# Adding the weights by DMA onto the negated high part, for every second weight piece of the mixer phases

## The chip, the cores and the metric

The kernel runs on one core of a Trainium2 chip. The metric is the time of one execution on the device in microseconds (us): 961.36 us in the median of three runs (961.18 to 961.63). Beside these times there is one profiled execution, whose trace gives the instructions of each engine: TensorE (PE, with its weight loads PEld), VectorE (DVE), ScalarE (ACT), GpSimd (POOL) and SyncE (SP, which only issues DMAs here).

## The reference

Two layers of a decoder trunk work on 272 positions (16 learned ones and 256 of the sequence) of width 1024, all in float32. Cut to what matters:

```
for l in range(2):
    h = rms_norm(x, norm1_g[l])
    u = h @ w_in[l]                      # conv, q, kv, rope key, recurrence inputs, 3 x 1024 gates
    A = conv_module(u_conv) @ w_conv_out[l]     # GLU, causal depthwise conv k=31, layer norm, swish
    B = mla(c_q, c_kv, k_rope) @ w_attn_out[l]  # causal attention, 8 heads
    C = hgrn2(q, f, i, g) @ w_hgrn_out[l]       # gated linear recurrence, in chunks, 4 heads
    mix = sig(gA) * A + sig(gB) * B + sig(gC) * C
    x = x + mix @ w_out[l]
    x = x + square(relu(rms_norm(x, norm2_g[l]) @ w_ff1[l])) @ w_ff2[l]
return x[:, 16:]
```

## The kernel before

Activations lie transposed in SBUF: 128 partitions of features by 272 columns of positions (256 in parts of the second layer). The weights stay in HBM and come in pieces of 128x1024 float32, 512 KiB each; one piece holds eight 128x128 blocks.

The large products keep the accuracy of float32 by three products of a shorter format, float32r. Every operand is split into a high part (the value rounded to float32r) and a low part (the value less the high part). `mm3` multiplies, for each block, high by high (L219), weights low by high (L220), and high by activations low (L221).

`piece` (L204) makes a weight piece ready in three steps. `fetch` (L104) loads it into a buffer `wraw` through SP's DMA queue (L106). ACT rounds it into `whi` (L209). DVE subtracts, `wraw` less `whi`, into `wlo` (L211). There are three `wraw` buffers and four each of `whi` and `wlo`. A buffer of `whi` or `wlo` is free again when the matmuls that read it are done, one of `wraw` when its last reader is done.

Each layer has two phases. In the mixer phase, `win_acc` multiplies 51 pieces of w_in (piece j = 0 is the rope key and goes another way; j = 1 to 7 are the latents and the recurrence queries, j = 8 to 27 the other inputs, j = 28 to 51 the 24 gate tiles). `merge_tile` multiplies 12 pieces of the three branch matrices (wbr), each piece serving two of its 24 tiles, scales by the gate (L996) and sums (L998). The other work of the mixers is written as four step generators: `latent_steps`, `hgrn_steps` (the recurrence, with the products of L840 and L844), `attention_steps` and `conv_steps` (the convolution, 31 taps for each of four channel groups on DVE, L931 and L935). A loop over a list of the dense tiles draws steps from them at fixed rates. The list is the 20 head tiles j = 8 to 27, 15 gate tiles, and then a merge tile and, as long as there are any, a gate tile by turns. Before the first merge tile of a branch its generator is run to its end.

In the second phase come 8 pieces of w_out, 32 of w_ff1 and 32 of w_ff2, with no other large work beside them.

Every engine works through its own instructions strictly in their order, and waits at the first whose inputs or buffer are not ready. This order is made when the program is built: a planner plays the program through with its own costs of each instruction and gives each engine, whenever it comes free, the ready instruction of the highest priority. Priority is the order of writing, moved ahead by `tc.high_priority`: by 500 for `piece`, by 300 to 400 for the steps of recurrence, attention and latents, by nothing for the convolution. So a change of one instruction can move others.

POOL does small things: memsets of the recurrence's buffers (`kl`, L799), copies (`qm`, L851) and powers for the norms (L238, L912). It issues no DMA.

Of the kernel before, what the change touches and what calls it, by code (L numbers as in the profile page):

```python
# [10 lines left out]
F32 = mybir.dt.float32  # L11
# [3 lines left out]
AF = mybir.ActivationFunctionType  # L15
# [24 lines left out]
NLAT = 8  # L40
# [46 lines left out]
def block_kernel(ctx, tc, xT_d, pp_d, cc_d, win_d, wuq_d, wukv_d, wbr_d, wout_d, wff1_d, wff2_d, out_d):  # L87
    nc = tc.nc
    pe, act, dve, pool = nc.tensor, nc.scalar, nc.vector, nc.gpsimd
    MUL, ADD, SUB = ALU.mult, ALU.add, ALU.subtract  # L90
# [13 lines left out]
    def fetch(src, n=1024):  # L104
        raw = wsp.tile([P, 1024], F32, name="wraw", tag="wraw")
        nc.sync.dma_start(out=raw[:, :n], in_=src[:, :n])  # L106
        return raw
# [3 lines left out]
    with tc.high_priority(offset=2 * AHEAD):  # L111
        nc.scalar.dma_start(out=pp, in_=pp_d)
        for j in range(4):
            nc.sync.dma_start(out=xT[:, 2 * j:2 * j + 2, :], in_=xT_d[:, 2 * j:2 * j + 2, :])
            if j == 0:
                first = {"kr": fetch(win_d[0, 0], KD * ROPE), "kv": fetch(win_d[0, 1])}
# [72 lines left out]
    def psum_acc():  # L189
        return ps_acc.tile([P, 512], F32, name="acc", tag="acc")  # L190
# [4 lines left out]
    def psum_hx():  # L195
        return ps_hx.tile([P, 512], F32, name="hx", tag="hx")
# [4 lines left out]
    def psum_sm():  # L201
        return ps_sm.tile([P, 512], F32, name="sm", tag="sm")

    def piece(src, raw=None):  # L204

        with tc.high_priority(offset=AHEAD):
            raw = raw or fetch(src)
            hi = wsp.tile([P, 1024], F32R, name="whi", tag="whi", bufs=4)
            act.copy(out=hi, in_=raw)  # L209
            lo = wsp.tile([P, 1024], F32R, name="wlo", tag="wlo", bufs=4)  # L210
            dve.tensor_tensor(out=lo, in0=raw, in1=hi.bitcast(F32), op=SUB)  # L211
        return hi, lo

    def split(hi, lo, src):
# [3 lines left out]
    def mm3(out, whi, wlo, xhi, xlo, start, stop):  # L218
        pe.matmul(out, whi, xhi, start=start, stop=False)  # L219
        pe.matmul(out, wlo, xhi, start=False, stop=False)  # L220
        pe.matmul(out, whi, xlo, start=False, stop=stop)  # L221
# [62 lines left out]
    def scale_input(xg, l, k):  # L284
# [16 lines left out]
                      in1=lb[:, 5, :].unsqueeze(1).broadcast_to([P, 2, HH]), op=MUL)  # L301
# [5 lines left out]
    for l in range(DEPTH):  # L307
# [33 lines left out]
        def unit(name, dt=F32):  # L341
            return t4.tile([P, HH, L], dt, name=name, tag="u")
# [22 lines left out]

        tiles = win_tiles()
        def win_acc(j, n0):
            hi, lo = piece(win_d[l, j], first["kv"] if l == 0 and j == 1 else None)
            xh, xl = xg if j < NLAT else (hhi, hlo)
            ps = psum_hx() if j < NLAT and j % 2 == 0 else psum_acc()  # L370
            for k in range(KD):
                o = k * P
                mm3(ps[:, :L - n0], hi[:, o:o + P], lo[:, o:o + P], xh[:, k, n0:], xl[:, k, n0:],
                    k == 0, k == KD - 1)
            return ps
# [22 lines left out]
        def head_tile(j):  # L398
            kind, i, _, _ = tiles[j]
            if kind == "kr":  # L400
                rope_keys(j)
                return
            n0 = T0 if kind in ("q", "g") else 0
            ps = win_acc(j, n0)[:, :L - n0]
            with tc.high_priority(offset=200):
                take(kind, i, ps, n0)
# [40 lines left out]
        def latent_steps():  # L447
# [44 lines left out]
            for g in range(2):  # L492
                uqhi, uqlo = piece(wuq_d[l, g])
                for h in range(4):
                    ps = psum_mx()[:, :L]
                    for j in range(2):
                        o = j * 512 + h * P
                        mm3(ps, uqhi[:, o:o + P], uqlo[:, o:o + P], cqhi[:, j, :], cqlo[:, j, :], j == 0, j == 1)
                    act.activation(out=msq_[:QK, h, :], in_=ps[:QK], func=AF.Square)
                    dve.tensor_tensor(out=qT[g][:, h, :], in0=ps, in1=csg, op=MUL)  # L500
                    yield
                with together():
                    for h in (3, 2, 1, 0):
                        pe.matmul(sums[32 * h:32 * h + 32, :L], sel96[:QK, g, :], msq_[:QK, h, :], start=(g == 0), stop=(g == 1))
                yield
# [3 lines left out]
            for w in qtiles:  # L509
# [10 lines left out]
                                     in1=heads(ra[:, 1, q0:3]), op0=MUL, op1=MUL)  # L520

            ukhi, uklo = piece(wukv_d[l])
            kT = [unit(f"kT{g}") for g in range(2)]
            vv = [half(f"vv{w}", "vv", 3) for w in range(3)]
# [449 lines left out]
        mix = {}  # L974

        def gate_tile(i):

            ps = win_acc(N_HEAD_TILES + i, T0)
            gates[i] = gp.tile([P, L], F32, name="gate", tag="gate")
            act.activation(out=gates[i][:, :N], in_=ps[:, :N], func=AF.Tanh, scale=0.5)  # L980

        def merge_tile(i):
            b, m = divmod(i, KD)
            yh, yl = ys[BRANCHES[b]]
            if i == 0:
                mix["sum"] = [unit(f"mix{j}") for j in range(2)]
            if i % 2 == 0:
                mix["w"] = piece(wbr_d[l, i // 2])
            bhi, blo = mix["w"]
            ps = (psum_acc, psum_hx, psum_hx)[b]()  # L990
            for k in range(4):
                o = (i % 2 * 4 + k) * P
                mm3(ps[:, :N], bhi[:, o:o + P], blo[:, o:o + P], yh[:, k, T0:], yl[:, k, T0:], k == 0, k == 3)
            g, total = gates[i], mix["sum"][m // 4][:, m % 4, :N]
            with tc.high_priority(offset=AHEAD):
                dve.scalar_tensor_tensor(out=total if b == 0 else g[:, :N], in0=g[:, :N], scalar=1.0, in1=ps[:, :N], op0=ADD, op1=MUL)  # L996
            if b > 0:
                dve.tensor_tensor(out=total, in0=total, in1=g[:, :N], op=ADD)  # L998
            if b == 2:
                if m == 0:  # L1000
                    mix["hi"] = actp.tile([P, KD, L], F32R, name="mhi", tag="ahi")
                    mix["lo"] = actp.tile([P, KD, L], F32R, name="mlo", tag="alo")
                act.activation(out=mix["hi"][:, m, T0:], in_=total, func=AF.Copy, scale=0.5)
                dve.scalar_tensor_tensor(out=mix["lo"][:, m, T0:], in0=total, scalar=0.5, in1=mix["hi"][:, m, T0:].bitcast(F32),
                                         op0=MUL, op1=SUB)
# [3 lines left out]
        for i in range(3 * KD):  # L1009
            dense.append((merge_tile, i))  # L1010
            if i + NGATE < 3 * KD:
                dense.append((gate_tile, i + NGATE))
# [193 lines left out]
```

## Time and profile before

| | |
|---|---|
| three runs | 961.18, 961.36, 961.63 us |
| the profiled execution | 961.29 us, of which the span from its first to its last instruction is 959.5 us |
| granted TensorE clock | 0.991 of full speed over the span |
| PE busy | 931.0 us, 97% |
| DVE busy | 716.5 us, 75% |
| ACT busy | 526.3 us, 55% |
| POOL busy | 50.7 us, 5% |
| DMA | 149.16 MB, HBM read 146.91 MB |

Times in the rows are in us unless they stand as ns. Matmuls overlap, so "PE busy" can be full while their number per us still varies. A line such as "out<-in x276 | busy, mean ns | idle <-releaser" gives a group of instructions by the program's names, their count, their busy time in all, the mean of one, and the idle time of the engine just before them with what ended it. Layer 0's mixer phase lies at about 0 to 276 us, layer 1's at about 480 to 752 us.

### The profile page before, as it was taken

The numbers are of one execution on the slowest core, as the hardware profiler recorded it, in microseconds if no ns is written. First come the engines' busy times: TensorE is split into PE (matmuls) and PEld (weight loads), VectorE is DVE, ScalarE is ACT, GpSimd is POOL, SyncE is SP. The second block draws the span as 40 slices with busy tenths as digits, with TensorE's granted clock in tenths as the row PEclk, the third lists the DMA queues.
The fourth block names the chain that finished last, engine by engine and source line by source line (L and its number), as shares of the span: only waits on it lengthen the run. The fifth ranks groups of instructions, "written<-read, shape, count | busy, mean of one in ns | idle before, by whom it ended". The sixth has DMA issues, their size and how long they took to land. (4 is left out here: it accounts for less than half of the span.)

```text
span 959.5 us, 18623 instructions
## 1 busy us (share of the span) xinstructions
PE 931.0 (97%) x7474; PEld 896.2 (93%) x7474; DVE 716.5 (75%) x1348; ACT 526.3 (55%) x945; POOL 50.7 (5%) x87
## 2 busy tenths in 40 slices
PE   6999999899999999999999999997998999999998
PEld 6899999779999999999999889896897999999998
DVE  7799999976887766555557998999668887665552
ACT  6467665554546555544445587665444566663331
POOL 3004000000000000000010021000000000000000
PEclk9999999989999999999999999998999999999999
DMA  8454433414445555555454444333144466555661
GB/s 264 131 176 140 147 133 111 133 34 142 163 148 178 194 176 177 176 176 176 160 172 158 141 145 155 130 132 113 67 146 163 155 195 199 179 190 187 198 203 56
DMA packets 42422, 149.16 MB, mean 155 GB/s; under 512 B 4704, under 2 KB 6368, under 8 KB 42336
## 3 DMA queue, kind: packets, MB, share of 16 engines
q1 hardware_dynamic: 40608, 146.10, 46.2%
q10 hardware_dynamic: 1728, 1.88, 0.6%
q8 instruction: 58, 0.95, 0.4%
q14 instruction: 28, 0.23, 0.1%
HBM read 146.91 MB, written 1.05 MB: 154 GB/s over the span
## 5 line engine op out<-in xcount | busy, mean ns | idle before, releaser
L209 ACT CAST whi<-wraw 128x1024 fp32r<-128x1024 f32 x276 | 289.3, 1049 | 340.4 <-PE acc L221 191.2
L211 DVE TENSOR_TENSOR wlo<-wraw,whi 128x1024 fp32r<-128x1024 f32 x276 | 337.6, 1223 | 167.0 <-ACT whi L209 165.4
L219 PE MATMUL acc<-hhi,whi 128*128 128x272 f32 (+1 forms) x704 | 205.1, 292 | 2.3 <-ACT scrahi L417 1.6
L221 PE MATMUL acc<-hlo,whi 128*128 128x272 f32 (+1 forms) x704 | 202.7, 289 | 0.2 <-DVE hlo L216 0.2
L220 PE MATMUL acc<-hhi,wlo 128*128 128x272 f32 (+1 forms) x704 | 202.2, 287 | 0.0
L219 PEld LDWEIGHTS acc<-hhi,whi 128*128 128x128 f32 x704 | 132.6, 188 | 6.6 <-ACT scrahi L417 1.8
L221 PEld LDWEIGHTS acc<-hlo,whi 128*128 128x128 f32 x704 | 132.4, 188 | 2.5 <-issue 0.9
L220 PEld LDWEIGHTS acc<-hhi,wlo 128*128 128x128 f32 x704 | 132.6, 188 | 1.2 <-issue 0.4
L935 DVE SCALAR_TENSOR_TENSOR cacc<-hpad,pph,cacc 128x272 f32<-128x272 f32 (+1 forms) x240 | 111.0, 485 | 0.7
L220 PE MATMUL acc<-xhi,wlo 128*128 128x272 f32 (+1 forms) x256 | 73.4, 287 | 0.0
L220 PE MATMUL hx<-xhi,wlo 128*128 128x272 f32 (+1 forms) x256 | 73.2, 286 | 0.0
L221 PE MATMUL acc<-xlo,whi 128*128 128x272 f32 (+1 forms) x256 | 73.1, 286 | 0.0
L221 PE MATMUL hx<-xlo,whi 128*128 128x272 f32 (+1 forms) x256 | 72.9, 285 | 0.0
L220 PE MATMUL hx<-fhi,wlo 128*128 128x272 f32 (+1 forms) x256 | 72.9, 285 | 0.0
L220 PE MATMUL acc<-fhi,wlo 128*128 128x272 f32 (+1 forms) x256 | 72.9, 285 | 0.0
L219 PE MATMUL acc<-fhi,whi 128*128 128x272 f32 (+1 forms) x256 | 72.8, 284 | 0.0
L219 PE MATMUL hx<-fhi,whi 128*128 128x272 f32 (+1 forms) x256 | 72.8, 284 | 0.0
L221 PE MATMUL acc<-flo,whi 128*128 128x272 f32 (+1 forms) x256 | 72.7, 284 | 0.0
L221 PE MATMUL hx<-flo,whi 128*128 128x272 f32 (+1 forms) x256 | 72.7, 284 | 0.0
L219 PE MATMUL acc<-xhi,whi 128*128 128x272 f32 (+1 forms) x256 | 72.7, 284 | 0.0
L219 PE MATMUL hx<-xhi,whi 128*128 128x272 f32 (+1 forms) x256 | 72.7, 284 | 0.0
L221 PEld LDWEIGHTS acc<-xlo,whi 128*128 128x128 f32 x256 | 48.3, 189 | 0.1
(375 smaller groups left out, 2097.3 us busy)
## 6 DMA issues: line engine op xcount, KB each, us to landing
wraw<-in_wff_dram SPq DMA_DIRECT2D x128, 512.0 KB, 3.4
wraw<-in_win_dram SPq DMA_DIRECT2D x102, 512.0 KB, 3.4
wraw<-in_wbr_dram SPq DMA_DIRECT2D x24, 512.0 KB, 3.3
wraw<-in_wout_dram SPq DMA_DIRECT2D x16, 512.0 KB, 3.3
wraw<-in_wuq_dram SPq DMA_DIRECT2D x4, 512.0 KB, 3.2
xT<-in_xT_dram SPq DMA_DIRECT2D x4, 272.0 KB, 5.4
wraw<-in_wukv_dram SPq DMA_DIRECT2D x2, 512.0 KB, 3.7
out_dram<-xT ACTq DMA_DIRECT2D x8, 128.0 KB, 2.4
```

Source lines behind the costliest of these rows:

```text
L209: act.copy(out=hi, in_=raw)
L211: dve.tensor_tensor(out=lo, in0=raw, in1=hi.bitcast(F32), op=SUB)
L219: pe.matmul(out, whi, xhi, start=start, stop=False)
L220: pe.matmul(out, wlo, xhi, start=False, stop=False)
L221: pe.matmul(out, whi, xlo, start=False, stop=stop)
L935: dve.scalar_tensor_tensor(out=a, in0=hpad[:, c, T0 + k:T0 + k + N], scalar=hpar(l, "cw", c * CK + k), in1=a, op0=MUL, op1=ADD)
```

## The change

For some pieces DVE no longer subtracts. ACT writes the negated high part into `wlo`, and a DMA issued from POOL adds the weights from HBM onto it. These are the w_in pieces with odd j from 9 on (22 in each layer) and every second wbr piece (6 in each layer).

```diff
-    def piece(src, raw=None):
+    def piece(src, raw=None, adding=False):
+
 
         with tc.high_priority(offset=AHEAD):
             raw = raw or fetch(src)
             hi = wsp.tile([P, 1024], F32R, name="whi", tag="whi", bufs=4)
             act.copy(out=hi, in_=raw)
             lo = wsp.tile([P, 1024], F32R, name="wlo", tag="wlo", bufs=4)
-            dve.tensor_tensor(out=lo, in0=raw, in1=hi.bitcast(F32), op=SUB)
+            if adding:
+                act.activation(out=lo, in_=hi.bitcast(F32), func=AF.Copy, scale=-1.0)
+                nc.gpsimd.dma_start(out=lo, in_=src, accum_op=ADD)
+            else:
+                dve.tensor_tensor(out=lo, in0=raw, in1=hi.bitcast(F32), op=SUB)
         return hi, lo
...
         def win_acc(j, n0):
-            hi, lo = piece(win_d[l, j], first["kv"] if l == 0 and j == 1 else None)
+            hi, lo = piece(win_d[l, j], first["kv"] if l == 0 and j == 1 else None, j >= NLAT and j % 2 == 1)
...
             if i % 2 == 0:
-                mix["w"] = piece(wbr_d[l, i // 2])
+                mix["w"] = piece(wbr_d[l, i // 2], adding=i % 4 == 2)
```

## Rows read from the trace of the kernel before

**Rows 1.** The page's busy times, and DVE in 40 slices of 24 us.
```profile
PE 931.0 (97%) x7474; PEld 896.2 (93%) x7474; DVE 716.5 (75%) x1348; ACT 526.3 (55%) x945; POOL 50.7 (5%) x87
...
DVE  7799999976887766555557998999668887665552
```
**Rows 2.** Busy us (x instructions) by stretch: PE, PEld, DVE, ACT, POOL; clock, DMA share, GB/s.
```profile
120.00:150.00 30.00, 30.00 (x241) 27.78 (x240) 28.01 (x69) 19.36 (x50) 0.84 (x2) 1.00 0.37 123
170.00:202.00 32.00, 26.51 (x197) 21.91 (x195) 29.66 (x79) 18.59 (x49) 0.29 (x1) 0.89 0.27 89
552.00:576.00 24.00, 22.44 (x180) 21.49 (x179) 23.00 (x45) 21.68 (x37) 5.62 (x3) 1.00 0.42 142
656.00:680.00 24.00, 18.44 (x139) 15.36 (x139) 21.26 (x57) 12.97 (x34) 0.63 (x1) 0.79 0.19 66
720.00:744.00 24.00, 20.28 (x160) 19.03 (x159) 19.76 (x40) 11.81 (x19) 0.00 (x0) 1.00 0.45 156
744.00:768.00 24.00, 24.00 (x206) 24.00 (x205) 20.34 (x40) 13.33 (x23) 0.00 (x0) 1.00 0.50 158
```
**Rows 3.** PE's waits (total, times, longest) in 160 to 215, 640 to 700, 715 to 750.
```profile
PE hx L844 <- DVE k L840: 3.3, 1, 3.3
...
PE hx L844 <- DVE k L840: 2.8, 1, 2.8
...
PE hx L219 <- DVE gate L996: 2.7, 4, 0.9
PE hx L221 <- DVE yalo L216: 1.0, 2, 0.6
```
**Rows 4.** DVE's costliest groups in 170 to 202 us.
```profile
L935 DVE SCALAR_TENSOR_TENSOR cacc<-hpad,pph,cacc 128x272 f32<-128x272 f32 x39 | 17.7, 492 | 0.1
L211 DVE TENSOR_TENSOR wlo<-wraw,whi 128x1024 fp32r<-128x1024 f32 x5 | 6.1, 1222 | 1.2 <-ACT whi L209 1.2
```
**Rows 5.** The page's groups of the two split steps.
```profile
L209 ACT CAST whi<-wraw 128x1024 fp32r<-128x1024 f32 x276 | 289.3, 1049 | 340.4 <-PE acc L221 191.2
L211 DVE TENSOR_TENSOR wlo<-wraw,whi 128x1024 fp32r<-128x1024 f32 x276 | 337.6, 1223 | 167.0 <-ACT whi L209 165.4
```
**Rows 6.** The loads' DMA queue, the landings of wraw, and ACT's waits for them.
```profile
q1 hardware_dynamic: 40608, 146.10, 46.2%
...
DMA to landing us min/median/max: 2.8/3.4/6.6
...
ACT whi L209: 7.8, 11
```
**Rows 7.** POOL in order of time, 78 to 205 us: first and last of 11.
```profile
78.86 4.29 POOL L238 TENSOR_TENSOR rq<-rq,mhalf 128x24 f32<-128x24 f32 x1 [2.83 <-DVE rq L516]
...
203.67 1.00 POOL L912 TENSOR_TENSOR ss<-ss,mhalf 16x4 f32<-16x4 f32 x1 [16.98 <-DVE ss L911]
```
**Rows 8.** ACT's roundings with PE's first low-part matmuls of their pieces, by time.
```profile
27.13 1.05 ACT L209 CAST whi<-wraw 128x1024 fp32r<-128x1024 f32 x1 [0.85 <-DMA wraw<-in_win_dram]
...
39.76 0.29 PE L220 MATMUL acc<-hhi,wlo 128*128 128x272 f32 x1
...
45.70 1.05 ACT L209 CAST whi<-wraw 128x1024 fp32r<-128x1024 f32 x1
...
50.52 0.29 PE L220 MATMUL acc<-hhi,wlo 128*128 128x272 f32 x1
...
715.17 1.05 ACT L209 CAST whi<-wraw 128x1024 fp32r<-128x1024 f32 x1 [3.60 <-PE acc L221]
716.12 0.37 ACT L980 ACTIVATE gate<-acc 128x256 f32<-128x256 f32 x1
...
721.74 0.28 PE L220 MATMUL acc<-hhi,wlo 128*128 128x256 f32 x1
...
735.85 1.04 ACT L209 CAST whi<-wraw 128x1024 fp32r<-128x1024 f32 x1 [0.70 <-PE hx L221]
...
748.99 0.28 PE L220 MATMUL hx<-yahi,wlo 128*128 128x256 f32 x1
```

## The prediction

> **What bounds the kernel now.** I read the busy times first. TensorE (PE) works 931.0 of 959.5 us, 97%; VectorE (DVE) has 75% and ScalarE (ACT) 55%, but DVE is at 7 to 9 tenths in the slices of the two mixer phases [rows 1]. So the time can move in two ways only: PE's missing time can shrink, or PE can be made to wait where it does not wait now.
>
> Second, the table by stretches [rows 2]. In 120 to 150 us PE starts 241 matmuls in 30 us (8.03 per us) while DVE works 28.01 of 30: PE is the bound and DVE is nearly full beside it. In three stretches PE falls behind: 170 to 202 us (197 matmuls; at 8.03 per us 24.5 us of work, so 7.5 us lost), 656 to 680 us (139, 17.3 us, 6.7 lost) and 720 to 744 us (160; at the 206 in 24 us of the stretch behind it 18.6, so 5.4 lost). Together 19.6 us: the most that any help for DVE can bring there. In the first two the granted clock is at 0.89 and 0.79 of full speed, a mix of the 1.2 and 2.4 GHz levels while PE idled; that loss is inside the 19.6.
>
> Third, who PE waited for in these three stretches [rows 3]: a key product of the recurrence (L840) 3.3 and 2.8 us, merge and split results (L996, L216) 2.7 and 1.0 us, all of DVE: 9.8 us. The rest are ping-pong chains and waits for ACT. What DVE does in 170 to 202 us [rows 4] shows why not all 19.6 is DVE's fault: 17.7 of its 29.7 us are convolution taps (L935), which fill holes; splits (L211) are only 6.1.
>
> **What is removed.** Each layer has 22 changed pieces of win (odd j from 9 to 51) and 6 of wbr: 56 in all. Each loses one subtraction of 1.223 us [rows 5]: 68.5 us of DVE. What it is worth is read from the stretches: I credit the 9.8 us of PE's DVE waits (these stretches hold changed pieces, and 16 splits that vanish between 60 and 202 us, 19.6 us, are more than the 17.7 us of taps, so these can be out of the way before the chains run short of dense work). Bounds: nothing (the chains stay, an ACT step is added to them) and 19.6 us.
>
> **What is added on ACT.** A negated copy of 128x1024, 56 times. The nearest row is the rounding copy of that size, 1.049 us [rows 5]; 58.7 us in all, ACT from 526 to 585 us. ACT has room nearly everywhere (19.36 of 30 us busy in 120 to 150); where it has not is 552 to 576 us, 21.68 of 24 [rows 2]. Three changed pieces (j 19, 21, 23 of layer 1) put 3.15 us into 2.32 us of room: 0.8 us, and 3.15 if it all reaches PE, 0 if some other work fills in.
>
> **What is added on the DMA queue of GpSimd (POOL).** 56 issues that read the weights again: 512 KiB each, 29.4 MB on top of the loads' 146.10 [rows 6]. The DMA engines are busy 0.37 of 120 to 150 us [rows 2], so throughput hides it; without that cover the weight loads (3.4 us to landing) would come late, for which the rounding copies wait 7.8 us in all now. POOL itself has 11 operations between 78 and 204 us, the first of them the longest, 4.29 us, with long waits before them (16.98 us before the last) [rows 7]. An issue waits at the head of POOL's stream for its negated copy, and memsets of kl and powers queue behind it; conversely an issue put behind one of those waits sits there. With so few of them I cost both at nothing; each such collision would cost up to 4.3 us. The raw buffer is freed by the rounding copy, not by the subtraction, so the next load leaves SP's queue at least 1.2 us sooner; loads are not what PE waits for, so that is worth nothing.
>
> **The path that becomes late.** Before: rounding copy, then 1.22 us of DVE, then PE. After: rounding copy, negated copy, issue, landing, PE. PE needs the low part with the second matmul of a piece. The room is the time from the end of the rounding copy to that matmul. Four buffers for the high part set it: a copy starts only when a piece three places earlier is done. Examples [rows 8]: layer 0, j 11: 46.75 to 50.52, 3.8 us; layer 1, j 51: 716.22 to 721.74, 5.5. I took it so for all 56, from the first (28.18 to 39.76, 11.6 us) to the last (736.89 to 748.99, 12.1 us): one has 3.8, one 4.9, six 5.5 to 6.0, six 6.3 to 7.2, and 42 have 8.0 or more. Dense phases have 8 to 12, the merge phases 5.5 to 8.
>
> The price of the path: negated copy 1.05; one other ACT operation that slips in between, 0.37 as the gate's tanh at 716.12 [rows 8]; 0.1 for the hand-overs between the engines, my choice; and the landing. No row shows a DMA issued from POOL, nor one that adds. Bounds from the plain load: 3.4 us at its median, if adding and reading the old value cost nothing, and 6.6, its slowest landing [rows 6]. The add moves two operands: the load's packets took 46.2% of 959.5 us for 146.10 MB, so 1.59 us for 512 KiB; 3.4 + 1.59 = 5.0, and 0.3 for sharing the engines (0.37 busy, of half of 1.59): I take 5.3. Path 1.05 + 0.37 + 0.1 + 5.3 = 6.8 us (4.6 at the low bound without the slip, 8.1 at the high one).
>
> PE's loss is the sum of path less room over the pieces with less room. At 6.8: twelve pieces, 12.7 us. At 4.6: 0.8 us. At 8.1: 30.4 us. These losses add up, since a late piece pushes its followers, and their rooms move with it.
>
> The Trainium skill, DMA: Bandwidth & Descriptors, Anatomy of one DMA, puts a DMA issued from GpSimd at about 2.0 us plus bytes over 436 thousand, an estimate of 3.2 us here. By that alone the path would be 4.7 us, the loss 0.9, and the sum 953 us; no run here shows such a DMA, and the fit is not of an adding one.
>
> **The sum.** 12.7 + 0.8 - 9.8 = +3.7 us. The profiled execution took 961.29 us (span 959.5 and 1.8 around it), the median of three is 961.36: 965 us. All bounds at their worst: 30.4 + 3.2 - 0 = +33.6 (995); at their best 0.8 + 0 - 19.6 = -18.8 (942).
>
> **The rivals.**
> *DVE's relief wins (faster).* One mechanism: the landing is at or below 4.9 us, so that the path is 6.4 and the loss 8.5, less than 9.8 - 0.8. At a path of 6.0 the loss is 5.2; with 14 us of the 19.6 given back, because the taps are out of the tails, 961.3 + 5.2 + 0.8 - 14 = 953 us. For it: 17.7 us of taps in the 32 us before the merge, 42 of 56 pieces with 8 us of room, and the order on each engine is planned anew, so other ready matmuls may stand where a late piece stood. Against: the merge phases have nothing else to run.
> *The add is much slower.* At a path of 9 us (a landing of 7.5, beyond the bound) 23 pieces are late by 47.3 us in all: 961.3 + 47.3 + 0.8 - 9.8 = 1000 us. A mechanism of this kernel would be that the issue waits for DVE: an issue that must let a running DVE operation end waits up to 1.22 us behind a split, 0.49 behind a tap, and DVE works 28.01 of 30 us; path 8.0, loss 29, 982 us. The Trainium skill, SBUF — State Buffer, SBUF: two separate sides, says that GpSimd can't write descriptors while DVE holds the shared port in its two-port mode; no run here shows it. By that rule the operations with two inputs in SBUF, which are most of DVE's here, would not do it, so I give it little.
> *It evens out.* Loss and gain within 1.9 us: 961 us, with a path of 6.3 to 6.5.
> *It doesn't do what it says* can be excluded: the subtractions leave DVE's stream.
>
> **How the numbers follow.** A modest loss, 963 to 981 us: 0.39. Relief wins: 0.36. Much slower add: 0.12. Even: 0.13. Faster by over 0.2% (1.9 us, about what a measurement of this kernel can tell) 0.36, same 0.13, slower 0.51. The forecast is 965 us. Its own case spans 963 to 981; the range goes on through the even case and most of the faster one, down to 948, and into the slow one to 988: about 0.1 is left out on each side.
>
> **What would show it.** L211 220 times instead of 276, DVE near 648 us, ACT near 585, memory reads near 176 MB. Issue to landing of the add: 5.3 us. PE's waits: a new one for this DMA at the low part, some 13 us, in the merge phases (225 to 260, 700 to 735 us); the L840, L996 and L216 waits gone. The tap count in the last 30 us before each merge falls. I am wrong if PE shows no wait for the adding DMA (landing under 5, or work put in its place), if ACT's waits in the softmax chain grow, or if the three stretches lose as much as before.

## The result

The changed kernel takes 974.70 us in the median of four runs (972.91 to 978.66), the kernel before 961.27 us beside it (960.18 to 961.63): a ratio of 1.0139, 95% interval 1.0124 to 1.0155. So it is slower by 13.4 us. The forecast was 965 us with a range of 948 to 988 and 0.51 on slower. The sign came out and the place of the loss in part; both terms of the sum were too small.

### The profile page after: what moved, and what is told of

Same layout as the page of the kernel before. It is cut to its first block, busy times and chain, and to the rows that moved or that the text cites. A ratio compares the mean times of both kernels' runs of the same rounds, so it can differ in the third digit from the quotient of the medians.

```text
span 976.9 us, 18746 instructions
## 1 busy us (share of the span) xinstructions
PE 940.4 (96%) x7474; PEld 903.2 (92%) x7474; DVE 659.7 (68%) x1292; ACT 576.8 (59%) x1001; POOL 99.0 (10%) x143
## 3 DMA queue, kind: packets, MB, share of 16 engines
q0 software_dynamic: 8064, 29.36, 17.9%
## 4 chain that ended last, share of the span: by engine, by line
PE 83%; DMA 9%; ACT 4%; issue 3%; DVE 1%; POOL 0%; POOLq 0%; ACTq 0%; DVEq 0%
PE acc L225 16%; PE acc L224 16%; PE acc L226 16%; PE hx L225 8%; PE hx L226 8%; PE hx L224 8%; DMA wlo<-in_win_dram 6%; DMA wlo<-in_wbr_dram 2%; PE mx L639 1%; ACT whi L210 1%; PE hx L815 1%; ACT wlo L213 1%; DMA wraw<-in_win_dram 1%; PE sm L697 1%; PE pt L674 1%
## 5 line engine op out<-in xcount | busy, mean ns | idle before, releaser
L210 ACT CAST whi<-wraw 128x1024 fp32r<-128x1024 f32 x276 | 289.2, 1048 | 327.5 <-PE acc L226 181.7
L216 DVE TENSOR_TENSOR wlo<-wraw,whi 128x1024 fp32r<-128x1024 f32 x220 | 269.3, 1224 | 160.0 <-ACT whi L210 159.1
L225 PE MATMUL acc<-hhi,wlo 128*128 128x272 f32 (+1 forms) x704 | 208.4, 297 | 15.0 <-DMA wlo<-in_win_dram 14.9
L224 PE MATMUL acc<-hhi,whi 128*128 128x272 f32 (+1 forms) x704 | 210.3, 299 | 6.6 <-ACT scrahi L422 4.8
L226 PE MATMUL acc<-hlo,whi 128*128 128x272 f32 (+1 forms) x704 | 206.8, 295 | 0.0
L225 PEld LDWEIGHTS acc<-hhi,wlo 128*128 128x128 f32 x704 | 137.6, 196 | 19.5 <-DMA wlo<-in_win_dram 17.2
L224 PEld LDWEIGHTS acc<-hhi,whi 128*128 128x128 f32 x704 | 137.2, 195 | 11.6 <-ACT scrahi L422 5.5
L226 PEld LDWEIGHTS acc<-hlo,whi 128*128 128x128 f32 x704 | 137.1, 195 | 2.1 <-issue 1.5
L226 PE MATMUL acc<-xlo,whi 128*128 128x272 f32 (+1 forms) x256 | 73.3, 287 | 0.0
L226 PE MATMUL hx<-xlo,whi 128*128 128x272 f32 (+1 forms) x256 | 73.0, 285 | 0.0
L224 PE MATMUL acc<-fhi,whi 128*128 128x272 f32 (+1 forms) x256 | 72.9, 285 | 0.0
L224 PE MATMUL hx<-fhi,whi 128*128 128x272 f32 (+1 forms) x256 | 72.9, 285 | 0.0
L226 PE MATMUL acc<-flo,whi 128*128 128x272 f32 (+1 forms) x256 | 72.8, 284 | 0.0
L224 PE MATMUL acc<-xhi,whi 128*128 128x272 f32 (+1 forms) x256 | 72.8, 284 | 0.0
L226 PE MATMUL hx<-flo,whi 128*128 128x272 f32 (+1 forms) x256 | 72.8, 284 | 0.0
L224 PE MATMUL hx<-xhi,whi 128*128 128x272 f32 (+1 forms) x256 | 72.7, 284 | 0.0
L214 POOL DMA_DIRECT2D wlo<-in_win_dram x44 | 38.4, 874 | 240.1 <-ACT wlo L213 178.3
```

The costliest lines, as they stand in the source:

```text
L214: nc.gpsimd.dma_start(out=lo, in_=src, accum_op=ADD)
```

## The profile after

The profiled execution of the changed kernel is its longest, 978.66 us with a span of 976.9 and a mean granted clock of 0.988; the other three show 0.991, as the kernel before does. The diff moves line numbers by up to five: the rounding is now L210, the negated copy L213, the issue L214, the subtraction L216, the three matmuls L224 to L226.

The page of the changed kernel: busy times, DVE in 40 slices, queues, groups, and DMA issues with the median us to landing (compare [rows 1, 5, 6]).

```profile
PE 940.4 (96%) x7474; PEld 903.2 (92%) x7474; DVE 659.7 (68%) x1292; ACT 576.8 (59%) x1001; POOL 99.0 (10%) x143
...
DVE  7679699953577866655557876998526787675552
...
q1 hardware_dynamic: 40608, 146.10, 45.8%
q0 software_dynamic: 8064, 29.36, 17.9%
...
HBM read 176.27 MB, written 1.05 MB: 182 GB/s over the span
...
L210 ACT CAST whi<-wraw 128x1024 fp32r<-128x1024 f32 x276 | 289.2, 1048 | 327.5 <-PE acc L226 181.7
L216 DVE TENSOR_TENSOR wlo<-wraw,whi 128x1024 fp32r<-128x1024 f32 x220 | 269.3, 1224 | 160.0 <-ACT whi L210 159.1
...
L214 POOL DMA_DIRECT2D wlo<-in_win_dram x44 | 38.4, 874 | 240.1 <-ACT wlo L213 178.3
...
wraw<-in_win_dram SPq DMA_DIRECT2D x102, 512.0 KB, 3.8
wlo<-in_win_dram POOLq DMA_DIRECT2D x44, 512.0 KB, 5.9
wraw<-in_wbr_dram SPq DMA_DIRECT2D x24, 512.0 KB, 4.6
wlo<-in_wbr_dram POOLq DMA_DIRECT2D x12, 512.0 KB, 7.3
```

The subtractions fell from 276 to 220 and their time by 68.3 us, as the diff says; DVE's busy time as a whole fell by 56.8 us to 659.7 (648 was forecast), since ends of instructions that overlap are counted once. Three figures are new. The 56 adds take 17.9% of the 16 engines' span, 976.9 x 0.179 / 56 = 3.12 us each, where a load takes 1.59 by the prediction's reckoning. An add lands 5.9 us (win) or 7.3 us (wbr) after its issue began; over all 56 the landing is 5.2 us at least, 6.5 in the median and 9.0 at most. And the raw loads of wbr land after 4.6 us.

The same stretches as before (compare [rows 2]; same columns).

```profile
170.00:202.00 32.00, 32.00 (x258) 28.79 (x257) 26.47 (x70) 25.23 (x56) 3.88 (x5) 1.00 0.67 168
552.00:576.00 24.00, 21.60 (x154) 19.08 (x152) 20.33 (x44) 19.66 (x29) 6.43 (x4) 1.00 0.59 154
656.00:680.00 24.00, 24.00 (x210) 22.66 (x209) 22.08 (x60) 18.97 (x43) 2.00 (x3) 1.00 0.75 191
720.00:744.00 24.00, 19.32 (x139) 18.92 (x139) 8.85 (x15) 11.75 (x17) 4.09 (x5) 0.87 0.74 191
```

The two stretches ahead of the merges are full: 258 matmuls where there were 197, 210 where there were 139. The merge stretch is emptier, 139 after 160, though DVE now has 8.85 us of work there in place of 19.76. That is the trade in four rows.

These stretches are fixed in time, and the program has moved under them: the first merge matmuls of the two layers start at 201.93 and 675.61 us in the kernel before, at 210.58 and 689.41 here. The 32 and 24 us that end at them here, and the whole merge phase of layer 1 from there on, read the same way (before: 197 and 135 matmuls, and 732 in the 92.4 us from 675.6):

```profile
178.60:210.60 32.00, 32.00 (x259) 27.33 (x257) 21.55 (x50) 21.14 (x49) 3.60 (x4) 1.00 0.69 182
665.40:689.40 24.00, 24.00 (x212) 21.45 (x211) 17.96 (x43) 18.53 (x39) 2.23 (x3) 1.00 0.73 191
689.40:780.00 90.60, 82.61 (x657) 79.91 (x654) 49.83 (x97) 47.22 (x70) 10.94 (x13) 0.96 0.72 187
```

PE's waits in the whole execution (total, times, longest; compare [rows 3]).

```profile
PE acc L225 <- DMA wlo<-in_win_dram: 14.9, 9, 3.5
PE hx L400 <- DVE wkr L396: 7.4, 1, 7.4
PE acc L224 <- ACT scrahi L422: 4.8, 3, 2.4
PE hx L225 <- DMA wlo<-in_wbr_dram: 2.0, 3, 1.5
PE acc L224 <- ACT scrahi L415: 1.3, 1, 1.3
PE hx L224 <- DVE gate L1001: 1.3, 2, 0.7
```

The waits for the key product and for the split result have gone (the wait for `wkr` is at the start of the kernel, and was there before). In their place stand 16.9 us for adding DMAs, in 12 places: 11.0 us of it in the two merge phases, 5.4 in the head of layer 0.

The longest of them, from the timeline of 78 to 98 us (start, duration, engine, line, operation, and in brackets the idle time ahead):

```profile
81.01 1.06 ACT L213 ACTIVATE wlo<-whi 128x1024 fp32r<-128x1024 f32 x1
...
81.70 1.97 POOL L243 TENSOR_TENSOR ks<-ks,mhalf 128x8 f32<-128x8 f32 x1
...
83.65 4.16 POOL L243 TENSOR_TENSOR rq<-rq,mhalf 128x24 f32<-128x24 f32 x1
...
87.77 0.89 POOL L214 DMA_DIRECT2D wlo<-in_win_dram  x1
...
96.57 0.59 PE L225 MATMUL acc<-hhi,wlo 128*128 128x272 f32 x1 [3.53 <-DMA wlo<-in_win_dram]
```

The negated copy is done at 82.07, but POOL's stream has two powers, of 1.97 and 4.16 us, ahead of the issue, so the DMA starts at 87.77, lands 8.76 us later (the median is 6.5), and PE stands for 3.53 us. This is the collision that the prediction named at "up to 4.3 us" and costed at nothing.

What follows a wait, by three stretches around the merge wait that ends at 726.75 us (the columns of [rows 2]; the eighth figure is the granted clock):

```profile
722.00:727.70 5.70, 3.50 (x30) 3.29 (x29) 2.05 (x4) 1.33 (x2) 0.71 (x1) 1.00 0.91 250
727.70:731.10 3.40, 3.40 (x19) 3.40 (x18) 0.00 (x0) 0.00 (x0) 0.00 (x0) 0.50 0.07 29
731.10:738.00 6.90, 6.90 (x60) 6.90 (x60) 1.27 (x3) 4.29 (x6) 1.74 (x2) 1.00 0.59 132
```

After the idle time the granted clock is 0.50 for 3.4 us, the 1.2 GHz level: 19 matmuls in 3.4 us, where 60 follow in 6.9. The trace has seven such spells: four at waits for an adding DMA (38, 96, 728 and 741 us), two at waits for a recurrence input that ACT makes (`scrahi`, 55 and 577 us), one at the end. Four other waits of 1.3 to 1.6 us for adding DMAs (236, 249, 265 and 714 us) have none behind them. Before there were three, two of them at the waits of 3.3 and 2.8 us for the key product [rows 3].

## The experiments

All times are medians; the ratio, with its 95% interval, is to runs of the kernel before on the same chip (961.84 us in the median beside E1 to E4, 961.22 beside E5 to E8, 961.19 beside E9 to E12). Differences below are taken each to its own runs of before, so that the changed kernel stands at +13.4 us.

**E1. The relief alone.** The negated copy stays; the DMA goes.

```diff
                 act.activation(out=lo, in_=hi.bitcast(F32), func=AF.Copy, scale=-1.0)
-                nc.gpsimd.dma_start(out=lo, in_=src, accum_op=ADD)
```

> The DMA that adds is left out (the low part of the 56 pieces is then just the negated high part, so the output is not the reference's); the negated copies on ACT and DVE's relief stay. Late landing (my theory): PE's waits for the low part, 17 us in the profile after, vanish and the relief is kept, so 955 to 960 us, below the kernel before. Rival 1, ACT's 56 negated copies delay everything else: 970 to 975 us. Rival 2, the new order of the instructions is what costs: also 968 us or more.

Measured: 945.08 us, ratio 0.9828 [0.9812, 0.9845], a difference of -16.8 us. The two stretches ahead of the merges:

```profile
170.00:202.00 32.00, 31.79 (x253) 27.42 (x252) 19.40 (x38) 20.21 (x38) 1.00 (x1) 1.00 0.39 133
656.00:680.00 24.00, 23.99 (x201) 21.52 (x200) 13.53 (x23) 12.79 (x23) 2.01 (x2) 1.00 0.30 96
```

So the relief, with the cost of the negated copies already taken off, is worth 16.8 us, far more than the 9.8 - 0.8 = 9.0 of the prediction and than the run's own expectation. The mean clock of the profiled execution is 1.000, of the other three 0.998: part of the gain is the clock. Before it was 0.991 over 959.5 us, so clock spells cost 8.6 us at most, and here they are nearly gone. The price of the adding DMA is the rest of the way to the changed kernel: 13.4 + 16.8 = 30.2 us.

Where this price arises is shown by the first merge matmul of layer 0, in the kernel before, the changed kernel and E1:

```profile
201.93 0.39 PE L219 MATMUL acc<-ybhi,whi 128*128 128x272 f32 x1
...
210.58 0.49 PE L224 MATMUL acc<-ybhi,whi 128*128 128x272 f32 x1
...
193.09 0.39 PE L223 MATMUL acc<-ybhi,whi 128*128 128x272 f32 x1
```

The spans of the changed kernel and of E1 lie 35.6 us apart, and 17.5 of that is there by this matmul, though only 5.4 of the 16.9 us of waits for adding DMAs lie ahead of it. Three half-clock spells (38, 55 and 96 us) lie there too; what the rest is was not settled.

**E2. The adding DMA alone.** DVE also subtracts, into the raw buffer, so only its relief is undone.

```diff
             if adding:
                 act.activation(out=lo, in_=hi.bitcast(F32), func=AF.Copy, scale=-1.0)
                 nc.gpsimd.dma_start(out=lo, in_=src, accum_op=ADD)
-            else:
-                dve.tensor_tensor(out=lo, in0=raw, in1=hi.bitcast(F32), op=SUB)
+            dve.tensor_tensor(out=raw if adding else lo, in0=raw, in1=hi.bitcast(F32), op=SUB)
```

> The DMA path stays as in the changed kernel, and DVE subtracts for the 56 pieces as well (its result goes into the raw buffer and is read by nobody; the output is unchanged). So DVE's relief is undone alone. My theory: relief was worth about 10 us, so 982 to 990 us, and the tails before the merges (in the kernel before 170 to 202 and 656 to 680 us) lose PE time again. Rival, the relief was worth nothing: 973 to 977 us as the changed kernel.

Measured: 1001.91 us, ratio 1.042 [1.0396, 1.0444], above what was expected. DMA and negated copies together cost 40.1 us when DVE gets nothing back, and the relief gives back 26.7 of them. That is more than E1's 16.8. The run isn't a clean opposite: the subtraction holds the raw buffer longer, raw loads of wbr land after 5.5 us, and the waits for adding DMAs grow to 24.6. The two terms do not add.

**E3. A plain DMA in its place.** The same transfer overwrites.

```diff
-                nc.gpsimd.dma_start(out=lo, in_=src, accum_op=ADD)
+                nc.gpsimd.dma_start(out=lo, in_=src)
```

> The DMA from POOL's queue stays, but overwrites instead of adding (the low part is then the weights themselves, so the output is not the reference's). If adding, which moves two operands, makes the landing long: landing falls from 6.5 us to about 4.9 (one transfer of 1.59 us less) and the time to 962 to 968 us. Rival, issue by POOL and the second weight stream make it long: landing stays at 6 us or more and the time at 972 to 976 us.

Measured: 959.03 us, ratio 0.9972 [0.996, 0.9985]. Its queue and its DMA issues:

```profile
q0 software_dynamic: 8064, 29.36, 9.9%
...
wlo<-in_win_dram POOLq DMA_DIRECT2D x44, 512.0 KB, 4.5
...
wlo<-in_wbr_dram POOLq DMA_DIRECT2D x12, 512.0 KB, 5.0
```

The plain transfer takes 958.2 x 0.099 / 56 = 1.69 us of the 16 engines, the add 3.12: an add costs nearly two transfers. It lands in 4.6 us in the median over all 56 where the add takes 6.5, and PE's waits for it are 4.9 us in 5 places. Against the changed kernel it saves 13.4 + 2.8 = 16.2 us: so much of the 30.2 is the adding itself; the other 14.0 are what any second stream of weights on this path costs. The Trainium skill, Collectives: The Full Stack, The bandwidth ceiling, explains the halved rate of a reduce step between cores by an add that needs two source reads; the ratio here, 3.12 to 1.69, is 1.85 and fits that. The Trainium skill's fit in DMA: Bandwidth & Descriptors, Anatomy of one DMA, which gave 3.2 us in the prediction, falls short even of the plain transfer's 4.6 (3.4 at its fastest). The time lies below both expectations.

**E4, E7, E9. Which pieces.** Three choices of the adding pieces: the head pieces j = 9 to 41 (34 pieces), the merge phases' ones (j from 43 and wbr, 22 pieces), and only j = 25 to 41 (18 pieces).

```diff
-            hi, lo = piece(win_d[l, j], first["kv"] if l == 0 and j == 1 else None, j >= NLAT and j % 2 == 1)
+            hi, lo = piece(win_d[l, j], first["kv"] if l == 0 and j == 1 else None, NLAT <= j < 43 and j % 2 == 1)  # E4
+            hi, lo = piece(win_d[l, j], first["kv"] if l == 0 and j == 1 else None, j >= 43 and j % 2 == 1)         # E7
+            hi, lo = piece(win_d[l, j], first["kv"] if l == 0 and j == 1 else None, 25 <= j < 43 and j % 2 == 1)    # E9
-                mix["w"] = piece(wbr_d[l, i // 2], adding=i % 4 == 2)
+                mix["w"] = piece(wbr_d[l, i // 2], adding=False)                                                # E4, E9
```

> Only the win pieces before the merge phases (odd j 9 to 41, 34 in all) take the DMA path; the later 22 are subtracted by DVE again. My theory: PE's waits for late landings in the merge phases vanish, the tails stay relieved, ACT's crowd in layer 1 stays: 956 to 964 us, about the kernel before. Rival, what costs is spread over all changed pieces: 34 of 56 of the 13.4 us, 969 us.

> The complement of the run with the pieces before the merge phases: only odd win pieces from j 43 on and the 12 wbr pieces take the DMA path (22 of 56). Late landing: these have the smallest rooms and give almost no relief to the stretches before the merges, so 970 to 976 us. Rival, the loss is spread over all changed pieces: 22 of 56 of 13.4 us, 967 us.

> The adding form only for the odd head pieces from j = 25 to 41 of both layers (18 pieces); the other 38 go back to VectorE. If the cost of an added piece is set by the room that its matmuls leave it, these 18 land in time and only the relief is left: no wait for an adding DMA above 1 us in all, no half-clock spell behind one, 951 to 958 us. Rival: what the relief gives comes with the pieces that are now VectorE's again, and 18 pieces give nothing that shows: 960 to 963.

Measured: E4 962.87 us, 1.0013 [1.0003, 1.0022]; E7 966.76 us, 1.0054 [1.0039, 1.0069]; E9 950.58 us, 0.9889 [0.9875, 0.9904]. PE's waits in E4:

```profile
PE acc L225 <- DMA wlo<-in_win_dram: 5.7, 3, 4.2
PE acc L224 <- ACT scrahi L422: 4.8, 3, 2.4
```

in E7:

```profile
PE acc L225 <- DMA wlo<-in_win_dram: 6.3, 5, 2.5
PE hx L849 <- DVE k L845: 4.2, 2, 2.4
...
PE hx L225 <- DMA wlo<-in_wbr_dram: 2.3, 2, 2.0
```

(the waits for the key product are back, as its pieces relieve nothing ahead of the merges), and in E9, where none for an adding DMA is left (its longest and its only ACT wait over 1.5 us):

```profile
PE hx L400 <- DVE wkr L396: 7.4, 1, 7.4
...
PE acc L224 <- ACT scrahi L422: 1.6, 1, 1.6
```

E4 came as expected, and not at the 969 us of a loss spread evenly over the changed pieces. E7 came where that rival put it (967), 3 us below the theory's range. E9 came just below its range of 951 to 958.

The stretches ahead of the merges in E9:

```profile
170.00:202.00 32.00, 30.14 (x243) 25.38 (x242) 24.28 (x60) 20.69 (x50) 2.18 (x3) 1.00 0.38 116
656.00:680.00 24.00, 22.16 (x189) 18.80 (x189) 16.04 (x30) 12.73 (x30) 2.04 (x2) 1.00 0.26 88
```

E9 keeps most of the relief (243 and 189 matmuls, against 197 and 139 before and 253 and 201 in E1; in the 32 and 24 us up to each kernel's own first merge matmul 244 and 194, 197 and 135, 263 and 211) and pays nothing for landings: 10.6 us faster than the kernel before, and the version to keep. Its adds land no faster, 6.0 us in the median; they are hidden by the room of these pieces. The 16 pieces by which E4 differs from it, j = 9 to 23, cost 1.0 + 10.6 = 11.6 us: 5.7 of waits for the add, the longest of them, 4.2, again behind two powers on POOL, 3.2 more behind `scrahi`, and the clock spells behind these. The rest of the change's loss doesn't split so cleanly: E4's +1.0 and E7's +5.5 sum to 6.5 of the 13.4. The plan of every engine is made anew for each choice, and where the remaining 6.9 sit was not settled.

**E5, E8. A shorter path.** The negated copy is written straight from the raw weights, ahead of the rounding, so that the DMA can start one ACT operation earlier (E5 with all 56 pieces, E8 with E4's 34). The copy into the float32r tile rounds as it writes, so the low part comes out the same way.

```diff
             hi = wsp.tile([P, 1024], F32R, name="whi", tag="whi", bufs=4)
-            act.copy(out=hi, in_=raw)
             lo = wsp.tile([P, 1024], F32R, name="wlo", tag="wlo", bufs=4)
             if adding:
-                act.activation(out=lo, in_=hi.bitcast(F32), func=AF.Copy, scale=-1.0)
+                act.activation(out=lo, in_=raw, func=AF.Copy, scale=-1.0)
                 nc.gpsimd.dma_start(out=lo, in_=src, accum_op=ADD)
-            else:
+            act.copy(out=hi, in_=raw)
+            if not adding:
                 dve.tensor_tensor(out=lo, in0=raw, in1=hi.bitcast(F32), op=SUB)
```

> ACT writes the negated rounded weights straight from the raw piece, before the high part, so that the adding DMA is issued about 1.2 to 1.5 us earlier against the buffer's release; all 56 pieces, the same copies, the same DMAs. Late landing: the path from the release of a buffer to the landing shrinks by that much, PE's waits for the low part fall from 17 us to about 8 and the spells at half clock behind them get fewer, 962 to 968 us. Rival, the second stream of weights costs by its traffic and not by when it lands: 972 to 976 us.

> The negated copy first, and only the 34 pieces before the merge phases. Late landing: the few waits that are left there (6 us, one of them behind a power on POOL) shrink, so 953 to 959 us, below the kernel before. Rival: as the run with the high part first, 961 to 965 us.

Measured: E5 976.55 us, 1.0149 [1.0132, 1.0166]; E8 966.29 us, 1.0047 [1.0033, 1.0062]. Both expectations missed; PE waits 20.0 us for adds in E5. Its DMA issues:

```profile
wraw<-in_win_dram SPq DMA_DIRECT2D x102, 512.0 KB, 4.8
wlo<-in_win_dram POOLq DMA_DIRECT2D x44, 512.0 KB, 7.1
wraw<-in_wbr_dram SPq DMA_DIRECT2D x24, 512.0 KB, 6.2
wlo<-in_wbr_dram POOLq DMA_DIRECT2D x12, 512.0 KB, 8.0
```

The microsecond saved on ACT came back in the transfers: adds land in 7.1 and 8.0 us where they took 5.9 and 7.3, raw loads in 4.8 and 6.2 where they took 3.8 and 4.6, with the same bytes. So the landing is not a constant of the add; how long it takes depends on what runs beside it. The traces point to the raw loads: in the changed kernel 24 of the 56 adds were issued within 1.5 us of a raw load, and these land in 7.4 us in the median, the other 32 in 5.5; in E5 it is 55 of 56, with 7.3. The next raw load starts 0.7 us behind the add in the median there, 3.6 in the changed kernel. So the earlier issue moved nearly every add beside a raw load.

**E6. GpSimd subtracts.** The relief without any DMA.

```diff
             if adding:
-                act.activation(out=lo, in_=hi.bitcast(F32), func=AF.Copy, scale=-1.0)
-                nc.gpsimd.dma_start(out=lo, in_=src, accum_op=ADD)
+                pool.tensor_tensor(out=lo, in0=raw, in1=hi.bitcast(F32), op=SUB)
```

> POOL subtracts the 56 pieces in place of DVE, with no negated copy and no DMA. If the relief of DVE is the gain and a path of 2 to 4 us is short against the rooms of 5.5 us and more: no waits of PE for the low part, 940 to 948 us. Rival: POOL and DVE hold each other off, so DVE's splits and taps get longer than 1.22 and 0.49 us, and the time is 955 us or more.

Measured: 980.99 us, 1.0205 [1.019, 1.0221], as the rival had it. Two groups of its page:

```profile
L213 POOL TENSOR_TENSOR wlo<-wraw,whi 128x1024 fp32r<-128x1024 f32 x56 | 141.3, 2525 | 230.7 <-ACT whi L210 214.4
...
L939 DVE SCALAR_TENSOR_TENSOR cacc<-hpad,pph,cacc 128x272 f32<-128x272 f32 (+1 forms) x240 | 148.8, 643 | 1.0
```

The subtraction takes 2.53 us on POOL, and a tap on DVE 643 ns in the mean where it took 486 in the changed kernel: DVE is at 739.9 us, 23 more than before with 56 subtractions fewer. The Trainium skill, SBUF — State Buffer, SBUF: two separate sides, says that a DVE operation with two SBUF inputs and a GpSimd operation that reads SBUF lock one port pair against each other for a whole instruction; the longer taps agree. The 33 taps that overlap a subtraction on POOL took 1.65 us in the mean, the other 207 took 0.48. So this run does not price the relief alone.

**E10, E11, E12. More room.** A fifth buffer for `whi` and `wlo` fits only if the gate tiles get 7 buffers in place of 15. E10 is the changed kernel with 7 gate buffers, E11 has the fifth buffers too, and E12 is the kernel before with both.

```diff
-NGATE = 15
+NGATE = 7
-            hi = wsp.tile([P, 1024], F32R, name="whi", tag="whi", bufs=4)
+            hi = wsp.tile([P, 1024], F32R, name="whi", tag="whi", bufs=5)   # E11, E12; wlo too
```

> Control for the next run: the changed kernel with 7 gate buffers in place of 15, which frees SBUF and lets the planner place fewer gate tiles early. The late landings stay (12 to 20 us of waits for the adding DMAs), 970 to 985 us.

> As the control, with five buffers in place of four for the high and for the low part, so that a piece can start one piece earlier. If it is the room of four buffers against a path of 8.3 us from rounding to landing that makes pieces late, the waits for adding DMAs fall below 4 us, the half-clock spells behind them go, and the time is 15 to 28 us below the control: 947 to 965. Rival: pieces start when the written order or the raw loads let them and not when a buffer comes free, so that the fifth buffer changes less than 5 us.

> The kernel before (VectorE subtracts every piece) with the same 7 gate buffers and five weight buffers. If the relief of VectorE is worth its 17 us wherever the landing is hidden, this one stays 6 to 17 us slower than the run before it with the adding form. Rival: the fifth buffer gives VectorE the same slack that the relief gives, and the two come out within 4 us.

Measured: E10 1008.39 us (1007.09 to 1013.99), E11 974.40 (973.11 to 975.34), E12 984.49 (983.79 to 985.19). E10 and E11 lie above the expected levels, since 7 gate buffers cost more than was thought; all three are slower than the kernel before, and the comparisons among them are what counts. PE's waits for the adds in E10:

```profile
PE hx L225 <- DMA wlo<-in_wbr_dram: 14.6, 4, 5.6
PE acc L225 <- DMA wlo<-in_win_dram: 11.1, 10, 3.6
```

and in E11:

```profile
PE hx L225 <- DMA wlo<-in_wbr_dram: 4.7, 4, 2.1
PE acc L225 <- DMA wlo<-in_win_dram: 2.9, 4, 1.1
```

The fifth buffer takes the waits from 25.7 to 7.6 us, while the landing itself does not get shorter (5.8 us in the median in E10, 6.8 in E11). So it is room, not speed, that lets an add be hidden. It saves 34.0 us in all, more than the 18.1 of these waits; how much of the rest a fifth buffer gives without any add wasn't tried. With this room the change wins: E11 is 10.1 us below E12, the same kernel with DVE subtracting, as expected, and their runs don't overlap.

## Why the prediction came out as it did

**What bounds the kernel** held: PE's missing time shrank where DVE was late and grew where the new transfer was late.

**Removed work** was counted right (68.3 us of subtractions, 68.5 forecast) and credited too low. The step that failed is the 9.8 us, taken from PE's waits that name DVE; its upper bound of 19.6, all that the three stretches lost, was nearer. E1 gives 16.8 net of ACT. The reason given for a low credit, that taps fill DVE's holes anyway, pointed the wrong way: taps in the 30 us before the first merge matmul fell from 37 and 36 (the two layers) to 25 and 32 (25 and 30 in E1), so part of them had been work that was late. And with the stalls went the half-clock spells, up to 8.6 us, which the 19.6 held and the 9.8 did not.

**ACT** took 576.8 us (585 forecast), the copies 1.058 us each (1.049). Its crowd in layer 1 cost what was forecast, as far as E1 tells: with the negated copies alone one wait of 2.4 us for `scrahi` stands where the kernel before had one of 1.6. The changed kernel has a second one, of 2.3 us at 578.2 us, and a half-clock spell of 6.8 us beside the two. This second wait is in E3 and E4 too, and not in E1, E2 or E9: the copies alone do not make it, what does was not shown, and the sum had no term for it.

**The landing** is the term that was sized worst. The path from the rounding's end to the landing is 8.3 us in the median over the 56 pieces, where 6.8 was taken and 8.1 was the upper bound. Its parts: the negated copy starts 0.19 us behind the rounding (0.53 in the mean; 0.37 taken), lasts 1.06, the hand-over to POOL is 0.30 (0.1 taken), and the landing 6.5 (5.3). The step that failed in the landing is its base, the 3.4 us of a load from SP's queue: a plain DMA from POOL's queue lands after 4.6 us in E3, 0.53 of it the issue (0.33 on SP). What adding puts on top was sized well, 6.5 - 4.6 = 1.9 us where 1.59 + 0.3 was taken.

The rule of room less path gave the count and not the pieces: 12 late pieces were forecast and 12 waits came, which is in part luck. They cost 16.9 us where 12.7 were forecast, 11.0 of them in the merge phases, where its list of signs placed them. But with the path as it was measured, 8.3 us, the rule gives more than the 30.4 us of its bound of 8.1, nearly twice what came, since rooms changed with the new order. The piece with the least room, layer 0's j 11 with 3.8 us, did not wait at all (PE waits for no add between 38 and 79 us), and layer 0's j 9, with 11.6 us of room [rows 8], waited 1.3.

That the 30.4 lies close to the 30.2 that the add costs by E1 is chance too; these are not 30 us of waiting. At a clock of 0.991 in the timed runs, spells cost up to 8.8 us, at E1's 0.998 up to 1.9, and the L422 waits for `scrahi` are 2.4 us longer than E1's: 16.9 + 6.9 + 2.4 = 26.2. The other 4.0 are not accounted for.

**POOL's stream at nothing** was wrong once and dearly: the 3.5 us of the longest wait, and 4.2 in E4. Three other issues were held for 1.2 to 1.8 us, and PE waited for none of them.

**Throughput at nothing** was wrong in part: with DMA at 0.74 of the merge stretch [rows 2: 0.45], raw loads of win and wbr land 0.4 and 1.3 us later (3.4 and 3.3 before), and E5 shows that it feeds back on the adds. For the rounded raw loads PE hardly waited.

**The rivals.** Relief wins at a short landing: E3, with a landing of 4.6, is 2.8 us faster than before, which fits the point of decision (4.9); but gain and loss were both sized at about half, so that the point came out right does not bear the two terms out. The issue that waits for DVE is refuted: POOL's issue takes 848 to 1056 ns over all 56, however busy DVE is.

So both terms came out at about half of what they are: 9.0 us of gain and 12.7 of loss forecast, 16.8 and 30.2 measured. That the errors offset each other in part is luck, and the forecast still lay 9.7 us low.

## What to carry to other kernels

Moving work from a busy engine to a DMA pays where the consumer leaves more room than the whole path takes, counted to the landing and with the issue's own time and its queue; choose the pieces by their room, as E9 did, and not by parity. Cost a stall at more than its length: here six spells of 3.4 us or more at half the clock stand beside waits of 1.3 to 3.5 us, while four waits of 1.3 to 1.6 have none; and by the same token removing stalls returned more than the waits that were listed. An accumulating DMA is to be reckoned as nearly two transfers on the engines.

## What had not been expected of the hardware

An add of 512 KiB takes 3.12 us of the 16 DMA engines, a plain transfer from the same queue 1.69; their issues take 0.85 and 0.53 us of POOL. The landing of the same add moved between 5.0 and 11.0 us over the runs (fastest and slowest in E10), and in the changed kernel its median was 7.4 us for the adds issued within 1.5 us of a raw load and 5.5 for the others. POOL's subtraction slowed DVE's taps from 486 to 643 ns in the mean, all of it in the taps that overlap one.
